# The last two modulation groups of layer 1 move from TensorE products to VectorE row sums

## The chip, the core and the metric

The kernel is written for one NeuronCore of a Trainium2 chip. TensorE (PE) multiplies matrices, VectorE (DVE) and ScalarE (ACT) work on elements, GpSimd (POOL) does some elementwise work too, and SyncE (SP) issues almost all transfers. The metric is the device time of one execution of the whole program in microseconds (us), lower being better; it is compared as the median of several executions.

## What is computed

One step of a small two-layer network over 384 tokens of width 1024: 128 context tokens and 256 latent tokens. In each layer six vectors are made from a conditioning vector, once for the context and once for the latents, and they shift, scale and gate the token stream:

```python
mod_ctx = (jax.nn.silu(c_ctx) @ w_mod[l] + b_mod[l])[None, :]
mod_lat = jax.nn.silu(c) @ w_mod[l] + b_mod[l]
...
def layer(x, mod, p, latent, kc, vc):
    sh1, sc1, g1, sh2, sc2, g2 = [m[:, None, :] for m in jnp.split(mod, 6, axis=-1)]
    h = layer_norm(x) * (1 + sc1) + sh1
    z = h @ p["w_in"] + p["b_in"]
    ...
    merged = ga * a_attn + gc * a_conv + gf * a_f
    x = layer_norm(ALPHA * x + g1 * (merged @ p["w_o"]), p["ln1_g"], p["ln1_b"])
    h = layer_norm(x) * (1 + sc2) + sh2
    u = dwconv(h @ p["w_up"], p["ffn_conv_w"], p["ffn_conv_b"])
    ug, uv = jnp.split(u, 2, axis=-1)
    x = layer_norm(ALPHA * x + g2 * ((jax.nn.silu(ug) * uv) @ p["w_down"]), p["ln2_g"], p["ln2_b"])
```

The kernel calls sh1 and sc1 group A, sh2 and sc2 group B, and g1 and g2 group G. A group of one layer is two half groups of 1024 x 1024 weights (4 MB each). `w_mod` is used for two vectors alone, so each of its 48 MB is read for very little arithmetic.

## The kernel before

All matrix products run with both operands split into a rounded part and a remainder (`whi`, `wlo`), so each product is three matmuls (`mm3`, L196 to L198). A weight block comes from memory as a `raw` tile of 1 MB (3 buffers); ScalarE rounds one half of it (`whi`, L179) and VectorE subtracts to get the remainder (`wlo`, L180), with 5 buffers of each. TensorE reads them from there.

A layer is `mixing`, then the output projection with its close, then the feed-forward loop. `mixing` runs three branches of eight steps each, in the order Fourier, attention, convolution. A step makes one gate tile (24 matmuls into a `ps` tile) and one branch tile (into an `acc` tile), and VectorE multiplies the two (L562). In the last two branches GpSimd adds the product to the merged sum (L563), and in the last one ScalarE and VectorE split that sum for the output projection (L566, L567). VectorE also runs the depthwise convolution (L785, 62 instructions a layer) and parts of the softmax in the first branches.

Modulation groups come in two ways. On TensorE (`mod_stream`, `mod_products`, L217) a group is 32 small matmuls, 64 records in the trace, in 4 steps of 16 records; they stream the weights past the two conditioning columns (`cpad`); its weights come as 32 tiles of 256 KB in `s2` buffers. On VectorE (`mod_rows`, L315) the transposed weights come as 8 tiles of 512 KB per half group, and each tile is multiplied with each of the two conditioning rows and summed along the row, two instructions a tile. The tiles pass through two `s4` buffers (of 8), and the transfer into a buffer is issued when the row sums that read it are done. Before, group A of layer 1 is made that way inside layer 0's feed-forward loop, all else on TensorE; layer 1's groups G and B run on TensorE inside layer 1's `mixing`. The conditioning rows are broadcast from a small scratch in memory, `cscr`, which setup writes.

The code is written in one order, and a scheduler fixes the order of each engine's instructions; an engine then runs its own in that order, and waits at one hold up all behind it. SP's queue is such an order as well.

Of the kernel before, what the change touches and what calls it, by code (L numbers as in the profile page):

```python
# [13 lines left out]
ALU = mybir.AluOpType  # L14
AX = mybir.AxisListType

P = 128
D = 1024
KD = D // P
DEPTH = 2  # L20
# [57 lines left out]
class Net:  # L78
# [52 lines left out]
    def setup(self):  # L131
        nc, a = self.nc, self.a
        self.zeros = self.const("zeros", [P, P])
        nc.vector.memset(self.zeros, 0.0)
        self.busy(self.WARM)
        self.ident = self.const("ident", [P, P])
        make_identity(nc, self.ident)
        self.mhalf = self.const("mhalf", [P, 1])
        nc.gpsimd.memset(self.mhalf, -0.5)
        self.zero2 = self.const("zero2", [P, 2 * KD])  # L140
        nc.gpsimd.memset(self.zero2, 0.0)
        self.cpad = self.const("cpad", [P, KD, 32])
# [12 lines left out]
        self.gscr = self.dr.tile([DEPTH, 2, 2, D], F32, tag="gscr", name="gscr", bufs=1)  # L155
        self.xscr = self.dr.tile([3, P, D], F32, tag="xscr", name="xscr", bufs=1)

    def setup_late(self):
        nc, a = self.nc, self.a
        att = self.const("att", [P, 128 + 768])  # L160
        self.load(att, a["k_att"])
        self.rope = att[:, 0:128].rearrange("p (t s c) -> p t s c", t=2, s=2)
        self.mask = att[:, 128:896].rearrange("p (t k) -> p t k", t=2)
        self.kT = [[self.sb.tile([P, 512], F32R, tag=f"kT{v}{i}", name=f"kT{v}{i}", bufs=1) for i in range(2)]
                   for v in range(NKV)]
        self.upad = [self.const(f"upad{i}", [P, UP_W]) for i in range(2)]
        for u in self.upad:
            nc.gpsimd.memset(u, 0.0)
# [124 lines left out]
                dst = self.modcol[l][:, gi, v, ks].rearrange("p (i q) -> p i q", q=ns)  # L293
                nc.vector.tensor_tensor(dst, part, bias, op=ALU.add)

    def mod_rows(self, l, kind):

        nc, a = self.nc, self.a
# [3 lines left out]
        b0 = 3 if kind == "B" else 0  # L302
        tiles = [(j, k) for j in range(2) for k in range(KD)]
        sums = [self.sm(16) for _ in range(2)]

        def fetch(n):
            j, k = tiles[n]
            self.load(w[n % 2], a["w_modr"][l - 1, self.MODS[kind], j, k])

        fetch(0)  # L310
        fetch(1)
        yield
        for n, (j, k) in enumerate(tiles):
# [3 lines left out]
            if n + 2 < len(tiles):  # L317
                fetch(n + 2)
            if k == KD - 1:
                for v in range(2):  # L320
                    nc.vector.tensor_tensor(self.modcol[l][:, j + (2 if kind == "B" else 0), v, :],
                                            sums[j][:, v * KD:(v + 1) * KD], self.bmod[l][:, j + b0, :], op=ALU.add)
            yield

    def gate_bc(self, l, j):
        out = []
# [179 lines left out]
        self.b_out(l, 1, acc, z, bb)  # L506


    def mixing(self, l, first, hT, mods):
# [23 lines left out]
        merged, m_hl = [None] * KD, []  # L533
# [36 lines left out]

        if l + 1 < DEPTH:
            self.columns(l + 1)
        mods = self.mod_stream(mods)
# [18 lines left out]
        cb = self.conv_branch(l, cT)  # L592
# [249 lines left out]
    TAIL = 5  # L842
    NF = 4

    def layer(self, l, first, hT, mods):
        nc, a = self.nc, self.a
        m_hl = self.mixing(l, first, hT, mods)
# [5 lines left out]
        for u in range(KD // 2):  # L853
            for h, w in enumerate(self.row_halves(self.raw(a["w_o"][l, u]))):
                k = 2 * u + h
# [78 lines left out]
        for u in range(KF // 2):  # L934
            ws = []
            for v in range(2):
                if 2 * u + v * KF in pre:
                    ws.append([None, None])
                else:
                    ws.append(self.halves(self.col_halves(self.raw(a["w_u"][l, u, v]))))  # L940
            for h in range(2):
                i = 2 * u + h
                cg = up_tile(i, ws[0][h])
                th = self.g()
                nc.scalar.activation(th, cg, AF.Tanh)  # L945
                nc.vector.scalar_tensor_tensor(cg, th, 1.0, cg, op0=ALU.add, op1=ALU.mult)
                cv = up_tile(KF + i, ws[1][h])
                nc.vector.tensor_tensor(cg, cg, cv, op=ALU.mult)  # L948
                hi, lo = self.r(), self.r()
                nc.scalar.copy(hi, cg)  # L950
                nc.vector.tensor_tensor(lo, cg, f32(hi), op=ALU.subtract)  # L951
                gT[i] = (hi, lo)
                if u >= 2:
                    next(rows, None)
            if u >= 1:
                down(u - 1)
        down(KF // 2 - 1)
# [47 lines left out]
    def run(self):  # L1005
# [4 lines left out]
        self.columns(0)  # L1010
        for x in xhat:
            self.norm(x, x, D)
        mods = [[(0, "G"), (0, "B")], [(1, "G"), (1, "B")]]
        first, hT = xhat, self.new_hT(0)
        for l in range(DEPTH):
            first, hT = self.layer(l, first, hT, mods[l])


@with_exitstack
# [8 lines left out]
def layout(i):  # L1028
# [30 lines left out]
    modr = g[1:][:, :, :, [0, 1]].reshape(L - 1, D, 1, 2, KD, P).transpose(0, 2, 3, 4, 5, 1)  # L1059
    kvf = cat([w_in[:, :, C_K:C_CONV], w_in[:, :, C_F:C_G]], 2)  # L1060
    up = a["w_up"]
    out = {
# [33 lines left out]
```

## Time and profile before

| what | value |
|---|---|
| median of 3 runs | 1161.87 us (1161.85 to 1164.48) |
| the profiled execution, own time | 1162.13 us |
| its span in the trace | 1160.3 us |
| PE busy | 1139.3 us (98%) |
| DVE busy | 785.1 us (68%) |
| ACT busy | 522.9 us (45%) |
| POOL busy | 77.5 us (7%) |

The span runs from the first to the last instruction of the trace, and 1.8 us of the execution's own time lie outside it. A busy share is an average over stages that have different limits, so the rows further down are read by stage. A wait is put down to the engine that ended it.

### The profile page before, as it was taken

The page shows a single profiled execution, that of the slowest core. Times are in us where ns is not written, and L with a number is a line of the kernel's source. Part 1 is how long each engine was busy: PE and PEld are TensorE (multiplying, and loading weights), DVE is VectorE, ACT ScalarE, POOL GpSimd, SP SyncE. Part 2 cuts the span into 40 slices and gives each one's busy share as a digit, 9 for nine tenths or more (in the row PEclk, how much of TensorE's full clock was granted, in tenths as well). Part 3 has the DMA queues.
Part 4 walks back from the last instruction along what each step waited for, and adds up shares of the span by engine and source line. Part 5 has one row for each costly group of instructions (what it writes and reads, how often), then busy time and mean ns, then how long its engine had stood idle before and what let it go on. Part 6 is the DMA issues. An engine that isn't in the chain of part 4 may idle for free.

```text
span 1160.3 us, 16670 instructions
## 1 busy us (share of the span) xinstructions
PE 1139.3 (98%) x6569; PEld 1019.4 (88%) x6569; DVE 785.1 (68%) x1332; ACT 522.9 (45%) x875; POOL 77.5 (7%) x91
## 2 busy tenths in 40 slices
PE   8999999999999999999999999999999999999996
PEld 6788888898999999999958978889989999999995
DVE  5579965445799976666776799444477666555667
ACT  2457743242754344444372766233447444334440
POOL 1010001121100000000021000111110000000001
PEclk9999999999999999999999999999999999999998
DMA  9764567633366663343335364783427333333411
GB/s 362 295 205 145 167 229 271 231 141 127 128 236 206 229 206 139 109 136 119 110 122 216 118 218 155 277 313 109 146 73 251 112 114 141 113 142 109 146 37 55
DMA packets 47806, 195.95 MB, mean 169 GB/s; under 512 B 5552, under 2 KB 6608, under 8 KB 32624
## 3 DMA queue, kind: packets, MB, share of 16 engines
q1 hardware_dynamic: 47296, 194.10, 47.3%
q8 instruction: 52, 0.85, 0.3%
q10 hardware_dynamic: 432, 0.79, 0.2%
q14 instruction: 26, 0.21, 0.0%
HBM read 191.41 MB, written 3.45 MB: 168 GB/s over the span
## 4 chain that ended last, share of the span: by engine, by line
PE 84%; DVE 8%; ACT 2%; DMA 2%; POOL 1%; issue 1%; SPq 0%; POOLq 0%; DVEq 0%; ACTq 0%
PE ps L196 16%; PE ps L198 16%; PE ps L197 16%; PE acc L196 9%; PE acc L197 9%; PE acc L198 9%; PE acc L217 2%; PE acc L767 1%; DVE sm L372 1%; DVE wlo L180 1%; POOL sm L376 1%; DVE s L818 1%; DVE s L828 1%; PE acc L755 1%; ACT whi L179 1%
## 5 line engine op out<-in xcount | busy, mean ns | idle before, releaser
L180 DVE TENSOR_TENSOR wlo<-raw,whi 128x1024 fp32r<-128x1024 f32 x216 | 269.1, 1247 | 236.2 <-ACT whi L179 227.2
L196 PE MATMUL ps<-hT,whi 128*128 128x386 f32 (+1 forms) x1088 | 370.3, 340 | 1.8 <-ACT g L548 1.5
L198 PE MATMUL ps<-hT,wlo 128*128 128x386 f32 (+1 forms) x1088 | 368.7, 339 | 0.0
L197 PE MATMUL ps<-hT,whi 128*128 128x386 f32 (+1 forms) x1088 | 368.4, 339 | 0.0
L179 ACT CAST whi<-raw 128x1024 fp32r<-128x1024 f32 x216 | 225.8, 1049 | 308.1 <-PE ps L197 211.4
L196 PEld LDWEIGHTS ps<-hT,whi 128*128 128x128 f32 x1088 | 205.2, 189 | 14.1 <-ACT whi L179 5.0
L197 PEld LDWEIGHTS ps<-hT,whi 128*128 128x128 f32 x1088 | 205.2, 189 | 2.7 <-issue 1.7
L198 PEld LDWEIGHTS ps<-hT,wlo 128*128 128x128 f32 x1088 | 205.3, 189 | 0.3 <-issue 0.3
L197 PE MATMUL acc<-wlo,r 128*128 128x512 f32 x360 | 142.3, 395 | 0.0
L196 PE MATMUL acc<-whi,r 128*128 128x512 f32 x360 | 142.1, 395 | 0.0
L198 PE MATMUL acc<-whi,r 128*128 128x512 f32 x360 | 141.9, 394 | 0.0
L198 PEld LDWEIGHTS acc<-whi,r 128*128 128x128 f32 x360 | 67.6, 188 | 16.2 <-DVE r L951 0.5
L196 PEld LDWEIGHTS acc<-whi,r 128*128 128x128 f32 x360 | 67.6, 188 | 14.9
L197 PEld LDWEIGHTS acc<-wlo,r 128*128 128x128 f32 x360 | 67.6, 188 | 14.4
L785 DVE SCALAR_TENSOR_TENSOR cv<-upad,cst,cv 128x399 f32<-128x399 f32 x120 | 70.1, 627 | 0.1
L376 POOL TENSOR_TENSOR sm<-sm,mhalf 128x1 f32<-128x1 f32 x21 | 23.0, 1099 | 612.4 <-DVE sm L375 611.7
L950 ACT CAST r<-g 128x386 fp32r<-128x386 f32 x44 | 22.7, 515 | 89.5 <-DVE g L948 89.5
L927 ACT ACTIVATE g<-ps,cst 128x386 f32<-128x386 f32 x84 | 56.3, 670 | 0.0
L930 DVE SCALAR_TENSOR_TENSOR g<-ps,cst,g 128x385 f32<-128x385 f32 x84 | 52.0, 619 | 2.3
L928 DVE SCALAR_TENSOR_TENSOR g<-ps,cst,g 128x385 f32<-128x385 f32 x84 | 51.6, 614 | 0.2
L563 POOL TENSOR_TENSOR g<-g,g 128x384 f32<-128x384 f32 x32 | 35.8, 1118 | 181.8 <-DVE g L562 173.3
L945 ACT ACTIVATE g<-g 128x386 f32<-128x386 f32 x44 | 23.2, 527 | 45.2 <-DVE g L930 45.2
(185 smaller groups left out, 1353.0 us busy)
## 6 DMA issues: line engine op xcount, KB each, us to landing
raw<-w_u SPq DMA_DIRECT2D x44, 1024.0 KB, 4.8
s<-w_mod SPq DMA_DIRECT2D x128, 256.0 KB, 4.4
raw<-w_g SPq DMA_DIRECT2D x24, 1024.0 KB, 7.8
raw<-w_d SPq DMA_DIRECT2D x22, 1024.0 KB, 4.9
raw<-w_mod SPq DMA_DIRECT2D x8, 1024.0 KB, 9.5
raw<-w_o SPq DMA_DIRECT2D x8, 1024.0 KB, 4.8
s<-w_modr SPq DMA_DIRECT2D x16, 512.0 KB, 4.2
s<-w_z SPq DMA_DIRECT2D x8, 512.0 KB, 9.7
```

The lines of the kernel that those rows point to most:

```text
L179: self.nc.scalar.copy(hi, raw)
L180: self.nc.vector.tensor_tensor(lo, raw, f32(hi), op=ALU.subtract)
L196: mm(ps, lh, rh, start=first, stop=False)
L197: mm(ps, lh, rl, start=False, stop=False)
L198: mm(ps, ll, rh, start=False, stop=last)
L217: self.nc.tensor.matmul(ps[32 * i:32 * i + 32, 0:n], self.cpad[:, k, :], src[k, i], start=ks[0] == 0 and k == ks[-1], stop=ks[-1] == KD - ...
L376: nc.gpsimd.tensor_tensor(mv[:, 3:4], mv[:, 2:3], self.mhalf, op=ALU.pow)
L563: nc.gpsimd.tensor_tensor(merged[m], merged[m], gt, op=ALU.add)
L785: nc.vector.scalar_tensor_tensor(c, u[:, i:i + CV_W], w, c, op0=ALU.mult, op1=ALU.add)
L927: nc.scalar.activation(c, ps, AF.Identity, bias=cols["ffn_b"][:, i:i + 1], scale=w[1])
L928: nc.vector.scalar_tensor_tensor(c[:, 1:NPAD], ps[:, 0:NPAD - 1], w[0], c[:, 1:NPAD], op0=ALU.mult, op1=ALU.add)
L930: nc.vector.scalar_tensor_tensor(c[:, 0:NPAD - 1], ps[:, 1:NPAD], w[2], c[:, 0:NPAD - 1], op0=ALU.mult, op1=ALU.add)
```

## The change

Layer 1's groups B and G are no longer made on TensorE. `mod_rows` now takes a list of half groups; half of group B joins group A in layer 0's feed-forward loop, and the other half of B and both halves of G (24 tiles, 48 row sums) are made while layer 1's attention and convolution branches run. `paced` spreads the tiles over the steps of a loop. A half of group G ends with a transpose on TensorE, a copy on ScalarE and a store into the scratch that the gate's broadcast reads. The write of `cscr` is issued later, in `setup_late`.

```diff
-        nc.sync.dma_start(self.cscr.rearrange("v (k p) -> (v k) p", p=P), ch)
+        self.silu = ch
...
     def setup_late(self):
+        nc.sync.dma_start(self.cscr.rearrange("v (k p) -> (v k) p", p=P), self.silu)
...
-    def mod_rows(self, l, kind):
+    def mod_rows(self, units):
...
-        tiles = [(j, k) for j in range(2) for k in range(KD)]
+        tiles = [(n, k) for n in range(len(units)) for k in range(KD)]
...
             for v in range(2):
-                nc.vector.scalar_tensor_tensor(prod, w[n % 2], 1.0, cb[v], op0=ALU.mult, op1=ALU.mult,
-                                               accum_out=sums[j][:, v * KD + k:v * KD + k + 1])
+                nc.vector.scalar_tensor_tensor(prod, w[i % 2], 1.0, cb[v], op0=ALU.mult, op1=ALU.mult,
+                                               accum_out=sums[n][:, v * KD + k:v * KD + k + 1])
+            if i + 2 < len(tiles):
+                fetch(i + 2)
...
+                if kind == "G":
+                    pt = self.psum("acc")[0:2 * KD, 0:P]
+                    nc.tensor.transpose(pt, sums[n], self.ident)
+                    row = self.kk()[0:2 * KD, :]
+                    nc.scalar.copy(row, pt)
+                    nc.sync.dma_start(self.gscr[l, j].rearrange("v (k p) -> (v k) p", p=P), row)
...
+    def paced(self, units, slots):
+
+        steps = self.mod_rows(units) if units else iter(())
+        need, done = len(units) * KD + 1, [0, 0]
+
+        def step():
+            done[0] += 1
+            while done[1] * slots < need * done[0]:
+                done[1] += 1
+                next(steps, None)
+
+        return step
...
+        step_rows = self.paced(rows, 14)
...
         for i, _ in enumerate(branch(1, 0, "w_a", 4, aT, lambda: values(3))):
             next(cb, None)
+            step_rows()
             if i % 2:
                 mod()
         for i, _ in enumerate(branch(2, 1, "w_c", 2, cT, lambda: [None for _ in cb])):
+            step_rows()
...
-        rows = self.mod_rows(l + 1, "A") if l + 1 < DEPTH else iter(())
+        step_rows = self.paced(rows, 17)
...
-        mods = [[(0, "G"), (0, "B")], [(1, "G"), (1, "B")]]
+        mods = [[(0, "G"), (0, "B")], []]
+        mix_rows = [[], [(1, "B", 1), (1, "G", 0), (1, "G", 1)]]
+        ffn_rows = [[(1, "A", 0), (1, "A", 1), (1, "B", 0)], []]
```

The first place is VectorE's order in layer 1's convolution branch. Before, it holds the gate product (L562, `g` times `acc`), the split of the merged sum (L567) and the remainders of the next weights (L180, `wlo`), and nothing else:

```order
L562 SCALAR_TENSOR_TENSOR g1333_7411<-g1333_7411,acc1334_7413 128x384
L567 SCALAR_TENSOR_TENSOR r1336_7423<-g1052_6016,r1335_7422 128x384
L180 TENSOR_TENSOR wlo1359_7559<-raw1357_7556,whi1358_7558 128x1024
L562 SCALAR_TENSOR_TENSOR g1338_7451<-g1338_7451,acc1339_7453 128x384
L567 SCALAR_TENSOR_TENSOR r1341_7463<-g1065_6087,r1340_7462 128x384
L180 TENSOR_TENSOR wlo1361_7563<-raw1357_7556,whi1360_7562 128x1024
```

Now the row sums (L317, into `s4`, from the tile `s41194` or `s41195` and a conditioning row) stand between them, and the numbers of the three older kinds are L586, L591 and L181:

```order
L181 TENSOR_TENSOR wlo1286_7352<-raw1284_7349,whi1285_7351 128x1024
L317 SCALAR_TENSOR_TENSOR s41193_6780,sm1197_6784<-s41195_6782,s41191_6776 128x1024
L586 SCALAR_TENSOR_TENSOR g1273_7278<-g1273_7278,acc1274_7280 128x384
L317 SCALAR_TENSOR_TENSOR s41193_6780,sm1197_6784<-s41195_6782,s41192_6778 128x1024
L591 SCALAR_TENSOR_TENSOR r1276_7290<-g1045_6027,r1275_7289 128x384
L317 SCALAR_TENSOR_TENSOR s41193_6780,sm1197_6784<-s41194_6781,s41191_6776 128x1024
L181 TENSOR_TENSOR wlo1288_7356<-raw1284_7349,whi1287_7355 128x1024
L317 SCALAR_TENSOR_TENSOR s41193_6780,sm1197_6784<-s41194_6781,s41192_6778 128x1024
```

About every second instruction of VectorE there is a row sum, from the last attention split on to the end of the branch.

The second place is TensorE at the end of that branch. Before, the last branch tile (`acc1384`) follows its gate tile (`ps1382`), and the output projection (`acc1391`) follows at once:

```order
L198 MATMUL ps1382_7696<-hT914_5332,wlo1376_7653 128x384
L196 MATMUL acc1384_7723<-r1271_7088,whi1330_7382 128x384
L197 MATMUL acc1384_7723<-r1272_7089,whi1330_7382 128x384
L198 MATMUL acc1384_7723<-r1271_7088,wlo1331_7383 128x384
L196 MATMUL acc1384_7723<-r1275_7097,whi1330_7382 128x384
L197 MATMUL acc1384_7723<-r1276_7098,whi1330_7382 128x384
L198 MATMUL acc1384_7723<-r1275_7097,wlo1331_7383 128x384
L196 MATMUL acc1391_7744<-whi1398_7752,r1335_7422 128x512
```

Now the transpose of the second half of group G (L330, from the row sums `sm1198`) stands ahead of the last two branch tiles (`acc1323` and `acc1328`):

```order
L197 MATMUL ps1326_7605<-hT915_5359,whi1319_7561 128x384
L198 MATMUL ps1326_7605<-hT916_5360,whi1319_7561 128x384
L199 MATMUL ps1326_7605<-hT915_5359,wlo1320_7562 128x384
L330 MATMUL acc1314_7550<-ident_96,sm1198_6785 16x128
L197 MATMUL acc1323_7592<-r1229_6993,whi1270_7249 128x384
L198 MATMUL acc1323_7592<-r1230_6994,whi1270_7249 128x384
L199 MATMUL acc1323_7592<-r1229_6993,wlo1271_7250 128x384
```

Twelve branch matmuls and the whole output projection have moved behind that transpose. The first half of G has such a transpose too, ahead of the second branch tile of the convolution branch.

The third place is VectorE at the same point of the change: the last row sums, then the two bias adds (L327) that the transpose waits for, and only then the last gate products:

```order
L317 SCALAR_TENSOR_TENSOR s41193_6780,sm1198_6785<-s41194_6781,s41192_6778 128x1024
L925 MEMSET ps1376_7896 128x2
L317 SCALAR_TENSOR_TENSOR s41193_6780,sm1198_6785<-s41195_6782,s41191_6776 128x1024
L925 MEMSET ps1377_7906 128x2
L317 SCALAR_TENSOR_TENSOR s41193_6780,sm1198_6785<-s41195_6782,s41192_6778 128x1024
L327 TENSOR_TENSOR sm1198_6785<-sm1198_6785,cst100_673 128x8 x2
L586 SCALAR_TENSOR_TENSOR g1322_7590<-g1322_7590,acc1323_7592 128x384
L586 SCALAR_TENSOR_TENSOR g1327_7630<-g1327_7630,acc1328_7632 128x384
```

All 48 row sums of layer 1's `mixing` thus stand ahead of the bias adds that release TensorE there.

## Rows read from the trace of the kernel before

**Rows 1.** The page, busy time, share of the span and instructions by engine.
```profile
PE 1139.3 (98%) x6569; PEld 1019.4 (88%) x6569; DVE 785.1 (68%) x1332; ACT 522.9 (45%) x875; POOL 77.5 (7%) x91
```

**Rows 2.** Windows of L217 alone: length, PE busy, PEld busy, clock, DMA.
```profile
667.70:732.80 65.10, 8.11 (x64) 1.47 (x64) 1.00 0.58 191
732.80:831.90 99.10, 7.70 (x64) 1.67 (x64) 1.00 0.58 210
```

**Rows 3.** Chain of waits around one modulation step: start, us, what.
```profile
755.94 1.85 PE acc L217 x16
757.80 0.37 PE ps L196
758.69 0.18 PE ps L197
```

**Rows 4.** Windows, all engines: PE, PEld, DVE, ACT, POOL busy, clock, DMA.
```profile
667.70:732.80 65.10, 65.05 (x420) 53.41 (x421) 58.42 (x129) 41.86 (x98) 0.53 (x1) 1.00 0.58 191
732.80:831.90 99.10, 98.71 (x585) 91.36 (x584) 45.74 (x68) 35.78 (x49) 17.61 (x18) 1.00 0.58 210
```

**Rows 5.** Timeline, DVE, layer 1's branches: start, length, instruction, wait.
```profile
722.87 1.23 DVE L180 TENSOR_TENSOR wlo<-raw,whi 128x1024 fp32r<-128x1024 f32 x1 [0.38 <-ACT whi L179]
724.01 0.63 DVE L785 SCALAR_TENSOR_TENSOR cv<-upad,cst,cv 128x399 f32<-128x399 f32 x1
...
732.23 0.56 DVE L648 TENSOR_TENSOR r<-acc,r 128x384 fp32r<-128x384 f32 x1 [1.72 <-ACT r L647]
...
788.00 0.68 DVE L282 COPY s<-acc 128x512 f32<-128x512 f32 x1
789.42 0.39 DVE L294 TENSOR_TENSOR md<-acc,cst 128x8 f32<-128x8 f32 x4 [0.75 <-PE acc L286]
...
831.39 0.55 DVE L562 SCALAR_TENSOR_TENSOR g<-g,acc 128x384 f32<-128x384 f32 x1
```

**Rows 6.** Timeline, PE, end of layer 1's convolution branch.
```profile
830.20 0.39 PE L196 MATMUL acc<-whi,r 128*128 128x512 f32 x1
```

**Rows 7.** Timeline, DVE, row sums in layer 0's feed-forward loop.
```profile
403.58 1.22 DVE L315 SCALAR_TENSOR_TENSOR s<-s,s 128x1024 f32<-128x1024 f32 x1
...
404.85 1.22 DVE L315 SCALAR_TENSOR_TENSOR s<-s,s 128x1024 f32<-128x1024 f32 x1
...
408.18 1.22 DVE L315 SCALAR_TENSOR_TENSOR s<-s,s 128x1024 f32<-128x1024 f32 x1
...
409.32 0.62 DVE L930 SCALAR_TENSOR_TENSOR g<-ps,cst,g 128x385 f32<-128x385 f32 x1
```

**Rows 8.** Tile view of w_modr: transfers from issue to landing.
```profile
DMA to landing us min/median/max: 3.6/4.2/9.4
```

**Rows 9.** Timeline, DVE, a remainder beside a GpSimd add.
```profile
740.90 1.89 DVE L180 TENSOR_TENSOR wlo<-raw,whi 128x1024 fp32r<-128x1024 f32 x1 [0.28 <-ACT whi L179]
```

**Rows 10.** Timeline, POOL, the add beside it and a slower one.
```profile
740.70 1.01 POOL L563 TENSOR_TENSOR g<-g,g 128x384 f32<-128x384 f32 x1 [5.05 <-DVE g L562]
...
811.07 1.87 POOL L563 TENSOR_TENSOR g<-g,g 128x384 f32<-128x384 f32 x1 [4.24 <-DVE g L562]
```

**Rows 11.** Windows, layer 0's feed-forward loop, with row sums and after them.
```profile
318.90:419.10 100.20, 99.87 (x548) 94.17 (x547) 96.80 (x156) 44.00 (x64) 0.00 (x0) 1.00 0.65 224
419.10:470.00 50.90, 50.90 (x267) 47.74 (x266) 31.09 (x45) 22.57 (x31) 0.00 (x0) 1.00 0.41 141
```

**Rows 12.** Timeline, SP, the first issues.
```profile
2.12 0.43 SPq L121 DMA_DIRECT2D s<-x_p  x1
5.53 0.33 SPq L154 DMA_DIRECT2D cscr<-kk  x1
```

**Rows 13.** Windows, the start: the last two columns are DMA share and GB/s.
```profile
6.00:7.00 1.00, 1.00 (x7) 1.00 (x7) 0.97 (x5) 0.00 (x0) 0.00 (x0) 1.00 0.76 277
```

**Rows 14.** Windows, TensorE's first gap: granted clock after POOL's column.
```profile
12.00:20.00 8.00, 4.03 (x66) 2.45 (x59) 5.79 (x21) 3.97 (x7) 0.55 (x1) 1.00 1.02 423
20.00:25.00 5.00, 5.00 (x42) 3.28 (x42) 1.38 (x4) 1.45 (x2) 0.00 (x0) 0.66 1.02 416
```

More of the change, by code (lines that the diff above doesn't have):

```diff
@@ L294, in mod_columns @@
                 nc.vector.tensor_tensor(dst, part, bias, op=ALU.add)
-    def mod_rows(self, l, kind):
-        nc, a = self.nc, self.a
+    def mod_rows(self, units):
+        nc = self.nc
         cb = [self.bcast(self.cscr[v]) for v in range(2)]
@@ L301, in mod_rows, with fetch @@
         w = [self.s4() for _ in range(2)]
-        b0 = 3 if kind == "B" else 0
-        tiles = [(j, k) for j in range(2) for k in range(KD)]
[L304 to L308, printed above, removed]
+        tiles = [(n, k) for n in range(len(units)) for k in range(KD)]
+        sums = [self.sm(16) for _ in units]
+        def fetch(i):
+            n, k = tiles[i]
+            l, kind, j = units[n]
+            self.load(w[i % 2], self.a["w_modr"][l, self.MODS[kind], j, k])
         fetch(0)
@@ L312, in mod_rows @@
         yield
-        for n, (j, k) in enumerate(tiles):
+        for i, (n, k) in enumerate(tiles):
             for v in range(2):
-                nc.vector.scalar_tensor_tensor(prod, w[n % 2], 1.0, cb[v], op0=ALU.mult, op1=ALU.mult,
-                                               accum_out=sums[j][:, v * KD + k:v * KD + k + 1])
-            if n + 2 < len(tiles):
-                fetch(n + 2)
+                nc.vector.scalar_tensor_tensor(prod, w[i % 2], 1.0, cb[v], op0=ALU.mult, op1=ALU.mult,
+                                               accum_out=sums[n][:, v * KD + k:v * KD + k + 1])
+            if i + 2 < len(tiles):
+                fetch(i + 2)
             if k == KD - 1:
+                l, kind, j = units[n]
+                bias = self.bmod[l][:, {"A": (0, 1), "B": (3, 4), "G": (2, 5)}[kind][j], :]
+                dst = sums[n] if kind == "G" else self.modcol[l][:, j + (2 if kind == "B" else 0)]
                 for v in range(2):
-                    nc.vector.tensor_tensor(self.modcol[l][:, j + (2 if kind == "B" else 0), v, :],
-                                            sums[j][:, v * KD:(v + 1) * KD], self.bmod[l][:, j + b0, :], op=ALU.add)
-            yield
+                    d = dst[:, v * KD:(v + 1) * KD] if kind == "G" else dst[:, v, :]
+                    nc.vector.tensor_tensor(d, sums[n][:, v * KD:(v + 1) * KD], bias, op=ALU.add)
+                if kind == "G":
[4 more added lines that the diff above has]
+                    nc.sync.dma_start(self.gscr[l, j].rearrange("v (k p) -> (v k) p", p=P), row)
+            yield
+    def paced(self, units, slots):
[7 more added lines that the diff above has]
+        return step
     def gate_bc(self, l, j):
@@ L506, in start_next, with mixing @@
         self.b_out(l, 1, acc, z, bb)
-    def mixing(self, l, first, hT, mods):
+    def mixing(self, l, first, hT, mods, rows):
         nc, a = self.nc, self.a
@@ L572, in mixing @@
             self.columns(l + 1)
-        mods = self.mod_stream(mods)
+        mods = self.mod_stream(mods) if mods else iter(())
         def mod():
             next(mods, None)
+        step_rows = self.paced(rows, 14)
         ci = conv_in()
@@ L843, with layer @@
     NF = 4
-    def layer(self, l, first, hT, mods):
+    def layer(self, l, first, hT, mods, mix_rows, rows):
         nc, a = self.nc, self.a
-        m_hl = self.mixing(l, first, hT, mods)
+        m_hl = self.mixing(l, first, hT, mods, mix_rows)
         gate = self.gate_bc(l, 0)
@@ L953, in layer @@
                 if u >= 2:
-                    next(rows, None)
+                    step_rows()
             if u >= 1:
@@ L1012, in run @@
             self.norm(x, x, D)
-        mods = [[(0, "G"), (0, "B")], [(1, "G"), (1, "B")]]
+        mods = [[(0, "G"), (0, "B")], []]
+        mix_rows = [[], [(1, "B", 1), (1, "G", 0), (1, "G", 1)]]
+        ffn_rows = [[(1, "A", 0), (1, "A", 1), (1, "B", 0)], []]
         first, hT = xhat, self.new_hT(0)
         for l in range(DEPTH):
-            first, hT = self.layer(l, first, hT, mods[l])
+            first, hT = self.layer(l, first, hT, mods[l], mix_rows[l], ffn_rows[l])
 @with_exitstack
@@ L1058, in layout @@
     mod = np.stack([g[:, :, :, [0, 1]], g[:, :, :, [3, 4]], g[:, :, :, [2, 5]]], 1)
-    modr = g[1:][:, :, :, [0, 1]].reshape(L - 1, D, 1, 2, KD, P).transpose(0, 2, 3, 4, 5, 1)
+    modr = mod.reshape(L, 3, D, 2, KD, P).transpose(0, 1, 3, 4, 5, 2)
     kvf = cat([w_in[:, :, C_K:C_CONV], w_in[:, :, C_F:C_G]], 2)
```

## The prediction

> **What bounds the kernel now.** The page comes first: PE is busy in 1139.3 of the 1160.3 us, DVE in 785.1 [rows 1]. Then the change has to be placed. The matmuls of L217 that it removes lie between 667.7 and 831.9 in layer 1's branches; I cut that at 732.8, where the split of the last attention tile ends on DVE [rows 2, 5]. The windows show PE full in both parts (65.05 of 65.1 and 98.71 of 99.1), DVE at 58.42 of 65.1 in the first and at 45.74 of 99.1 in the second [rows 4]. So TensorE is the bound in both, but in the first part DVE has 6.7 us to spare only, and in the second 53 us, into which 48 row sums are to go. The output projection begins at 830.20 [rows 6], 97.4 us after my cut; I make the sum from this distance.
>
> **What TensorE loses.** L217 is busy for 8.11 + 7.70 = 15.8 us [rows 2]. The chain shows a step of 16 records as 1.85 us, and the first matmul behind it as 0.37 where a usual one is 0.18 [rows 3]: 0.2 us more per step, 8 steps, 1.6. All in all some 17.5 us of TensorE's path, 9.5 in the first part and 8 to 9 in the second.
>
> First part: 9.5 can be won only if DVE follows. DVE's 58.42 lose the add of group G (about 0.7, the 128x512 copy's 0.68 [rows 5]) and 3.4 for two remainders and two convolution steps that now come behind the cut (2 x 1.14 and 2 x 0.55: start to start at 722.87, and 0.63 less the same overlap [rows 5]). That leaves 54.3. If DVE keeps all of its 6.7 us of idle time the part takes 61.0, a gain of 4.1; if it keeps none of what PE sets, 9.5. **I take −6.5**, nearer to the middle, since DVE's idle time there is made of short waits for ACT (0.38 and 1.72 in the rows) which shrink only in part.
>
> **What VectorE gains.** From the cut to G1's bias adds every row sum stands ahead of the transpose (L330) that TensorE must pass to reach the last two branch tiles and the output projection. So I add up DVE's time there. It has 45.74 now. Minus group B's copy and four adds, 1.1 (0.68 and 0.39 [rows 5]); minus two gate products and a split that are behind the bias adds now, 1.7 (0.55, 0.56); plus the 3.4 that came from the first part. The row sums: one is 1.22 us, and the next instruction starts 1.14 after it (408.18 to 409.32), but 1.27 when that is a row sum too (403.58 to 404.85) [rows 7]. In the new order six follow one another directly: 48 x 1.15 + 6 x 0.12 = 55.9. Six bias adds, 0.5. Sum 102.7.
>
> The Trainium skill, "VectorE: DVE Perf Modes", section "The DRAIN you can't avoid", says that the next operation does not start until the pipeline of the one before is empty, unless nothing holds it. By the rule without its exception a row sum would hold DVE to its printed end, and I estimate 5 us more for the 48. The rows at 408.18 show the exception (other work begins 0.08 us before the printed end), those of two row sums in a row the rule.
>
> Waits: a tile of 512 KB lands 3.6 to 9.4 us after its issue, 4.2 mostly [rows 8]. Two buffers with two row sums each give one tile per 2.3 us of row sums and about as much other work, so a landing of 4.2 fits mostly, not always where the order is dense; the first tile has no lead at all. **I take 4 us** of waits for tiles and for hand-offs from ACT and PE; the ends are 0, and 12 (two landings of 9.4 less 4.2, and a few of 0.5).
>
> GpSimd: the remainder at 740.90 takes 1.89 instead of 1.23, where an add of POOL had begun 0.2 us earlier, for 1.01 [rows 9, 10]; four remainders of this stretch show it, 2.6 us, and are in the 45.74. The reverse is there too: an add of POOL took 1.87 [rows 10]. So the two engines exclude each other, and whoever has begun finishes first. With DVE nearly full, 14 adds meet a busy DVE ahead of the bias adds. If all came first, DVE would stand still for 14 x 1.01 = 14.1, which is 11.5 more than now; if DVE never left a gap, 2.6 less. **I take +3.4**, nearer to the present state.
>
> The Trainium skill, "SBUF — State Buffer", section "Who interferes with whom", states that a DVE instruction with two inputs in SBUF contends with a GpSimd instruction that reads SBUF, and calls the shared ports an exclusive lock. The trace agrees (1.89 and 1.87); the full price by it is the upper end above.
>
> 102.7 + 4 + 3.4 = 110.1 to the bias adds. Then the transpose, 0.3, and twelve branch matmuls of 0.18 (the chain's usual one [rows 3]), 2.1: **112.5 us against 97.4, +15.1**. TensorE alone would need about 88 (97.4 less its own relief). It will therefore wait at this transpose for 10 us or more, the sum of all the earlier small waits included; and what is queued behind it is the rest of the branch and the whole output projection. The four removed transposes of B and the two new ones cancel within 1 us and lie inside.
>
> **Layer 0's loop.** With row sums it has PE at 99.87 of 100.2 and DVE at 96.80; behind them DVE has 31.09 in 50.9 [rows 11]. 16 more give 31.1 + 16 x 1.15 = 49.5, under 50.9. I take 0, as TensorE is full where the row sums run already. The cover is 1.4 us thin: a tile that lands 9.4 instead of 4.2 us after its issue [rows 8] could cost up to 5.
>
> **The clock.** Where TensorE had work for 4.03 of 8 us, the granted clock was 0.66 in the 5 us that followed [rows 14], that is partly the lower of its two levels. A wait of over 10 us could bring the same: 5 x 0.34 = 1.7. The ends are 0 and twice that.
>
> **The start.** SP issues the load of `x` at 2.12 and is done with it at 2.55; the store of `cscr` is issued at 5.53 [rows 12], so 3 us of SP's time pass in waiting for the vector it stores. That wait goes. But what comes behind lands in a DMA that is full: its share is 0.76 in the sixth to seventh us, the least behind that issue [rows 13], so 0.24 us are free. **−0.3**; the ends are −3.3 and 0.
>
> **Sum.** −6.5 + 15.1 + 0 + 1.7 − 0.3 = +10.0. The profiled execution took 1162.1, so 1172.1, and the median is 0.3 below it: **1172 us**.
>
> **Rivals.**
> 1. *VectorE keeps pace* (the other side). DVE streams with no gap, GpSimd waits instead, and tiles always land in time: 102.7 − 2.6 + 2.4 = 102.5 against 97.4, +5.1; the first part gives its whole 9.5, the clock nothing. 1162.1 − 9.5 + 5.1 − 0.3 = 1157; with the whole start, 1154. It decides when the last row sum ends less than some 101 us after the last attention split. For it: the order is fixed and dense, and row sums need no other engine. Against it: a remainder still waits for ACT's rounding and a gate product for PE, and the present loop with the same mix keeps 3.4 us of 100 idle [rows 11]. Chance 0.13.
> 2. *Break-even*: first part 8 to 9, the second +8 to +12: 1160 to 1165. Chance 0.15, most of it within 0.3%.
> 3. *GpSimd wins every time*: +8 on my sum, and late tiles with it: 1178 to 1186, up to 1192 with the whole 12 us of waits. For it: in this stretch it was mostly DVE that waited (four to one). Chance 0.14.
> 4. *Layer 0's loop falls behind* by the 5 us above: 1175 to 1178. Chance 0.05; it lies inside the likeliest range.
> 5. *Each row sum holds DVE for its whole length*, 1.27 from start to start as at 403.58 and not 1.14 [rows 7]: 42 x 0.12 = 5 us more, 1177. Against it stand 408.18 and most others. Chance 0.03. (It is the rule of "VectorE: DVE Perf Modes" in the Trainium skill.)
> 6. *TensorE's relief goes through whole*: 17.5 us less, 1144. It needs DVE to finish within 88 us work that sums to over 100. Chance 0.02.
>
> **How the numbers follow.** The forecast as worked out, 1166 to 1178, has 0.48; the rivals have the rest. A difference within 0.3% (3.5 us) could not be told from none by a measurement of this kernel. Faster by more is rival 1, rival 6 and little of 2: 0.15. Same is most of rival 2: 0.14. The rest, 0.71, is slower. The range 1158 to 1184 leaves out about a tenth at each end; the likeliest's own is 1166 to 1178.
>
> **What would show it.** L217 is gone from layer 1's branches, and the stretch to the last attention split is some 6 us shorter. DVE is busy in over 95% of the stretch behind it, with remainders or row sums of 1.9 us, or adds of 1.9 on POOL. PE has one wait of about 10 us or more at L330, released by DVE's bias adds (L327), with a lower granted clock behind it, and the output projection starts about 112 us after the last attention split. In layer 0's loop PE stays full. I am wrong if PE's time in the branches is spread over many waits for remainders (then DVE's lateness reaches TensorE everywhere, and the place of the transpose matters little), if TensorE reaches L330 with no wait (rival 1), or if PE loses time in layer 0's loop.

## The result

The changed kernel takes 1173.42 us (median of 4 runs, 1171.74 to 1174.37), the kernel before 1162.2 (1161.85 to 1164.48): a ratio of 1.0092, 95% interval 1.008 to 1.0104. Forecast were 1172, within 1158 to 1184. The profiled execution has a span of 1172.0 us against 1160.3.

The page, as [rows 1]: TensorE has 11.4 us less work, VectorE 73.6 us more, and the span is longer all the same.

```profile
PE 1127.9 (96%) x6439; PEld 1018.3 (87%) x6439; DVE 858.7 (73%) x1462; ACT 522.4 (45%) x877; POOL 86.6 (7%) x90
```

Where TensorE waits in layer 1's branches and output projection (us in total, times, longest):

```profile
PE acc L330 <- DVE sm L327: 21.0, 2, 17.9
PE ps L199 <- DVE wlo L181: 1.9, 2, 1.5
PE acc L828 <- DVE sm L399: 1.1, 1, 1.1
```

Both large waits are at the transposes of group G, 3.1 and 17.9 us, and the bias adds behind the row sums end them. All other waits are under 2 us.

Windows, all engines, columns as in [rows 4]: up to the last attention split, from there to the bias adds of G's second half, the 4.4 us behind them, and 50 us of layer 0's loop with row sums.

```profile
660.10:725.30 65.20, 64.48 (x394) 57.88 (x393) 60.73 (x141) 47.29 (x114) 0.00 (x0) 1.00 0.28 97
725.30:838.60 113.30, 88.67 (x496) 86.81 (x494) 104.99 (x166) 34.38 (x48) 26.74 (x17) 0.92 0.67 233
...
838.60:843.00 4.40, 4.38 (x16) 4.29 (x17) 0.99 (x2) 0.56 (x2) 1.01 (x1) 0.61 0.32 115
...
420.00:470.00 50.00, 50.00 (x263) 46.66 (x262) 46.86 (x75) 21.15 (x29) 0.00 (x0) 1.00 0.68 238
```

In the second window VectorE is busy for 105 of 113.3 us (93%) and TensorE for 88.7, the reverse of [rows 4]. Layer 0's loop keeps TensorE full.

VectorE's timeline in that window (start, length, instruction, wait): its beginning, a remainder beside a GpSimd add (the add is the last line), a wait for ScalarE, a wait for a tile, and its end.

```profile
724.73 0.56 DVE L675 TENSOR_TENSOR r<-acc,r 128x384 fp32r<-128x384 f32 x1 [0.90 <-ACT r L674]
725.20 1.21 DVE L181 TENSOR_TENSOR wlo<-raw,whi 128x1024 fp32r<-128x1024 f32 x1
726.34 0.55 DVE L586 SCALAR_TENSOR_TENSOR g<-g,acc 128x384 f32<-128x384 f32 x1
726.80 1.22 DVE L181 TENSOR_TENSOR wlo<-raw,whi 128x1024 fp32r<-128x1024 f32 x1
...
734.95 2.03 DVE L181 TENSOR_TENSOR wlo<-raw,whi 128x1024 fp32r<-128x1024 f32 x1
...
786.73 0.56 DVE L591 SCALAR_TENSOR_TENSOR r<-g,r 128x384 fp32r<-128x384 f32 x1 [1.46 <-ACT r L590]
...
835.87 1.23 DVE L317 SCALAR_TENSOR_TENSOR s<-s,s 128x1024 f32<-128x1024 f32 x1 [1.44 <-DMA s<-w_modr]
...
838.28 0.28 DVE L327 TENSOR_TENSOR sm<-sm,cst 128x8 f32<-128x8 f32 x2
...
733.97 1.93 POOL L587 TENSOR_TENSOR g<-g,g 128x384 f32<-128x384 f32 x1 [5.07 <-DVE g L586]
```

TensorE's timeline at the same point; the last row answers to [rows 6].

```profile
838.62 0.38 PE L330 MATMUL acc<-ident,sm 128*16 128x128 f32 x1 [17.93 <-DVE sm L327]
838.65 0.67 PE L197 MATMUL acc<-r,whi 128*128 128x384 f32 x1
839.12 0.52 PE L198 MATMUL acc<-r,whi 128*128 128x384 f32 x1
...
842.37 0.40 PE L197 MATMUL acc<-whi,r 128*128 128x512 f32 x1
```

The ledger of the span, after less before: layer 0's first branch matmul is 1.2 us earlier (62.87 against 64.07); layer 0's loop, from its first matmul to layer 1's first branch matmul, is as long as before (304.64 against 304.61); the last attention split ends 7.5 us earlier (725.29 against 732.79), so the first part won 6.3; from there the output projection starts after 117.1 us instead of 97.4, +19.7; from that start to the first matmul of layer 1's up-projection both take 58.44; TensorE's last matmul is 12.2 later, the span 11.7 longer.

### The profile page after: what moved, and what is told of

It is laid out like the page before. It is cut to its first block, busy times and chain, and to the rows that moved or that the text cites. A ratio compares the mean times of both kernels' runs of the same rounds, so it can differ in the third digit from the quotient of the medians.

```text
span 1172.0 us, 16503 instructions
## 1 busy us (share of the span) xinstructions
PE 1127.9 (96%) x6439; PEld 1018.3 (87%) x6439; DVE 858.7 (73%) x1462; ACT 522.4 (45%) x877; POOL 86.6 (7%) x90
## 4 chain that ended last, share of the span: by engine, by line
PE 35%; DVE 8%; issue 3%; DMA 2%; ACT 1%; POOL 1%; POOLq 0%; DVEq 0%; ACTq 0%
PE ps L197 7%; PE ps L199 7%; PE ps L198 6%; PE acc L197 4%; PE acc L198 4%; PE acc L199 4%; DVE s L317 3%; DMA s<-w_modr 2%; DVE wlo L181 1%; POOL sm L400 1%; PE acc L794 1%; PE acc L1018 1%; DVE s L845 0%; DVE sm L396 0%; DVE s L855 0%
## 5 line engine op out<-in xcount | busy, mean ns | idle before, releaser
L181 DVE TENSOR_TENSOR wlo<-raw,whi 128x1024 fp32r<-128x1024 f32 x216 | 268.9, 1247 | 184.8 <-ACT whi L180 180.3
L180 ACT CAST whi<-raw 128x1024 fp32r<-128x1024 f32 x216 | 225.9, 1049 | 308.6 <-PE ps L198 193.1
L317 DVE SCALAR_TENSOR_TENSOR s<-s,s 128x1024 f32<-128x1024 f32 x96 | 118.8, 1238 | 3.8 <-DMA s<-w_modr 3.5
L400 POOL TENSOR_TENSOR sm<-sm,mhalf 128x1 f32<-128x1 f32 x21 | 24.7, 1179 | 614.5 <-DVE sm L399 602.4
L587 POOL TENSOR_TENSOR g<-g,g 128x384 f32<-128x384 f32 x32 | 43.5, 1362 | 276.3 <-DVE g L586 272.0
```

What stands on the lines that cost most here:

```text
L180: self.nc.scalar.copy(hi, raw)
L181: self.nc.vector.tensor_tensor(lo, raw, f32(hi), op=ALU.subtract)
L317: nc.vector.scalar_tensor_tensor(prod, w[i % 2], 1.0, cb[v], op0=ALU.mult, op1=ALU.mult, accum_out=sums[n][:, v * KD + k:v * KD + k + 1])
L400: nc.gpsimd.tensor_tensor(mv[:, 3:4], mv[:, 2:3], self.mhalf, op=ALU.pow)
L587: nc.gpsimd.tensor_tensor(merged[m], merged[m], gt, op=ALU.add)
```

## The experiments

Each run is compared with the kernel before on the same chip, which takes 1162.2 to 1162.8 us there; the changed kernel's 1173.42 us, with which some runs are compared too, were measured beside 1162.2. A deferred finish means that a half of G leaves its row sums standing and gets transpose, copy and store at the place named; its transpose then goes into a `ps` tile and no longer into an `acc` tile. Where line numbers shift by a few, the lines are the same ones: the gate product is L586 or L593, a transpose of the normalised tokens L425 or L432, and so on.

**1. Both transposes late.**

```diff
         m_hl = self.mixing(l, first, hT, mods, mix_rows)
+        self.finish(0)
...
                 tail(t, n)
+        self.finish(1)
```

> All row sums stay where they are; only the two transposes of group G with their copies and stores move behind TensorE's last branch tile (first half) and behind the first part of the output projection (second half). Theory A (TensorE is held by the place of the transposes in its order): the waits of 3.1 and 17.9 us ahead of them go; the rest of the branch and the first three of eight steps of the output projection, 2.1 + 12.7 us, run in that time, and TensorE then waits some 6 to 8 us for the last splits of the merged sum, which still stand behind all row sums on VectorE. 1173.4 - 21 + 7 - 1 (clock) = about 1158, 1155 to 1162. Rival B (VectorE's sum sets the end wherever the transposes stand, through gate products, splits and remainders): the wait moves to another matmul and 1169 to 1174 remain.

Measured: 1174.63 us, ratio 1.0108 (1.0093 to 1.0123). The output projection did start at 822.50 instead of 842.37, but nothing came of it. TensorE's waits from there:

```profile
PE acc L432 <- ACT s L423: 10.6, 3, 6.1
PE acc L198 <- DVE g L593: 6.1, 1, 6.1
```

```profile
833.68 0.80 PE L198 MATMUL acc<-whi,r 128*128 128x512 f32 x1 [6.05 <-DVE g L593]
```

Six us are a wait as long as theory A foresaw, but not for a split: the output projection fills six `acc` tiles (three tiles of 128 tokens, two halves each), there are six buffers of `acc`, and the last one comes free only with the gate product (L593) of the last branch tile, which stands behind row sums. Over ten more are waits for normalised tokens in the close, which the kernel before hides. TensorE's own work from the start of the output projection to the up-projection also takes 63.5 us instead of the 57.9 of the changed kernel, at a granted clock of 0.92 against 1.00. The time is that of rival B, 0.6 above its range, but this edit has a cost of its own: the store of G's second half waited 10.3 us on SyncE's queue for the copy, ahead of loads of the close. That left the place of the transposes open.

**2. Half of B last.**

```diff
-        mix_rows = [[], [(1, "B", 1), (1, "G", 0), (1, "G", 1)]]
+        mix_rows = [[], [(1, "G", 0), (1, "G", 1), (1, "B", 1)]]
```

> The same 48 row sums and the same transposes; only the order of the half groups in layer 1's branches changes, both halves of G first and the half of B last, so that the last row sums release nothing that TensorE's branch needs. Theory A: the transposes stand earlier on both engines and cost some 3 to 6 us of waiting; the wait of 17.9 us goes, and some 6 to 8 us come back ahead of the output projection's last steps, as the splits still stand behind all row sums: 1159 to 1164. Rival B: 1169 to 1174, with the wait at the split of the merged sum instead.

Measured: 1164.27 us, ratio 1.0014 (1.0003 to 1.0024); 9 us of the 11 are gone. The same 48 row sums and both transposes are there. TensorE's waits:

```profile
PE acc L197 <- DVE g L586: 4.7, 2, 3.8
PE ps L199 <- DVE wlo L181: 2.7, 1, 2.7
...
PE acc L330 <- DVE sm L327: 1.6, 1, 1.6
PE acc L198 <- DVE wlo L181: 1.2, 1, 1.2
```

The output projection starts at 824.10 and waits in its first part for the last two gate products, which free its fifth and sixth `acc` tile, and for a remainder, not for the splits that theory A named; from its start to the up-projection it takes 67.0 instead of 58.4 us. The time is theory A's, 0.3 above its range.

**3. GpSimd's adds left out.**

```diff
-                        nc.gpsimd.tensor_tensor(merged[m], merged[m], gt, op=ALU.add)
+                        if l == 0:
+                            nc.gpsimd.tensor_tensor(merged[m], merged[m], gt, op=ALU.add)
```

> GpSimd's adds of the branch products to the merged sum are left out in layer 1, so the sum there holds the first branch alone. If their lock costs what the trace of the changed kernel shows (ten instructions of VectorE between the last attention split and the bias adds are longer by 0.5 to 0.8 us, 7 us in all), those bias adds come 7 us earlier after the last attention split (113.3 to about 106) and the time is 1166 to 1168. Rival: VectorE is held by rounding, tiles and TensorE just as long, and the time stays within 2 us of 1173.

Measured: 1166.94 us, ratio 1.004 (1.0025 to 1.0055), 6.5 less than the changed kernel. Windows from the last attention split to the bias adds, and the same remainder as at 734.95 above:

```profile
724.70:828.90 104.20, 86.67 (x496) 85.36 (x495) 97.65 (x168) 34.52 (x49) 3.53 (x3) 0.94 0.73 253
```

```profile
733.60 1.22 DVE L181 TENSOR_TENSOR wlo<-raw,whi 128x1024 fp32r<-128x1024 f32 x1
```

No instruction of VectorE is stretched any more; in the changed kernel ten were, by 7.6 us in all. VectorE's busy time falls by 7.3 and the stretch by 9.1 us; the other 1.8 are shorter waits (those for ScalarE's half of the split, 2.9, are gone, those for tiles grow from 3.0 to 5.3). The time is the one expected. The lock's price is thus shown, and that it reaches the end.

**4. Two tiles for all row sums.**

```diff
-            if i + 2 < len(tiles):
+            if i + 2 < len(tiles) and units[0][1] == "A":
```

> In layer 1's branches only the first two of the 24 tiles are loaded and every row sum reads these (the sums are not those of the weights). The three waits of VectorE for a tile there, 0.45 + 1.09 + 1.44 = 3.0 us, go. If VectorE's sum is what TensorE waits for, the time falls by 3, to about 1170.5; if a tile's wait only takes the place of a wait for ScalarE or TensorE behind it, by less than 1; if the transfers also slow the weights of the branches or VectorE itself, by 5 and more.

Measured: 1173.48 us, ratio 1.0097 (1.0082 to 1.0112). The waits for tiles are gone and the time is the same, as the second case has it. It settles less than it seems: the scheduler put the row sums earlier, the waits moved (13.2 us ahead of matmuls that need remainders, 5.5 at the transposes), and the last row sum starts at 837.00 against 837.13.

**5. Both transposes late, no store in the close.**

```diff
         m_hl = self.mixing(l, first, hT, mods, mix_rows)
+        self.finish(0)
...
+        self.finish(1)
         gate = self.gate_bc(l, 1)
```

> As the first experiment, but the second half of G gets its transpose, copy and store only ahead of the second gate's load at the end of layer 1's feed-forward loop, so that no store waits among the loads of the output projection's close. The row sums stay, in the order B, G, G. Theory A' (the place of the transposes costs what lies between the full relief and VectorE's lateness; the close was spoiled in the first experiment by the store on SyncE's queue): like the run with B last, 1162 to 1166, with some 10 to 14 us of TensorE waits left, for remainders, gate products and splits, and the store's 10 us wait on SyncE gone. Rival: the place is worth nothing and the order of the half groups gave what the second run gained: 1171 to 1175.

Measured: 1174.17 us, ratio 1.0098 (1.0081 to 1.0115). The output projection starts at 822.1, but the close's waits for normalised tokens (8.9 us) are there again without the store on the queue. Theory A' fell; the rival's time came out, not yet its reason.

**6. G's second half in layer 1's loop.**

```diff
-        mix_rows = [[], [(1, "B", 1), (1, "G", 0), (1, "G", 1)]]
-        ffn_rows = [[(1, "A", 0), (1, "A", 1), (1, "B", 0)], []]
+        mix_rows = [[], [(1, "G", 0), (1, "B", 1)]]
+        ffn_rows = [[(1, "A", 0), (1, "A", 1), (1, "B", 0)], [(1, "G", 1)]]
```

> The second half of G, used only at the end of layer 1's feed-forward loop, is made in that loop; 32 row sums remain in layer 1's branches (first half of G, then half of B), the transposes late. If VectorE's sum is the bound there: 16 x 1.15 and its share of locked adds less, 113.3 - 19.5 = 94 us against the 88 that TensorE needs, and the feed-forward loop hides the moved ones as layer 0's does: 1162.1 - 17.5 - 1.2 (start) + 5 = 1148, 1145 to 1152. Rival: remainders and gate products queue behind row sums however many there are, and the time stays over 1155; or layer 1's loop loses time (TensorE under 99% busy there).

Measured: 1155.69 us, ratio 0.9944 (0.9929 to 0.9959), 3.7 above the expected range and now faster than before. It is the rival's time, by 0.7, but not its reason: TensorE's longest wait in the branches is 1.6 us (gate activations), none there is for a remainder, and layer 1's loop shows no wait over 1.0.

**7. Row sums spread.**

```diff
+        mix_rows = [[], [(1, "G", 0)]]
+        ffn_rows = [[(1, "A", 0), (1, "A", 1), (1, "B", 0), (1, "B", 1)], [(1, "G", 1)]]
```

> All of A and B (32 tiles) in layer 0's loop, the first half of G in layer 1's branches (16 row sums), the second half in layer 1's loop. VectorE then has about 113.3 - 39 = 74 us of work where TensorE needs 88, so TensorE is the bound everywhere and its whole relief goes through: 1162.1 - 17.5 - 1.2 = 1143.4, 1141 to 1147. Rival: layer 0's loop, at 97% of VectorE for 50 us longer, falls behind: 1147 to 1152, with TensorE waits there.

Measured: 1149.9 us, ratio 0.9891 (0.9876 to 0.9906). Windows from the last attention split to the output projection:

```profile
725.90:816.60 90.70, 88.23 (x508) 87.53 (x508) 67.23 (x98) 34.41 (x48) 24.54 (x18) 1.00 0.48 164
```

TensorE is the bound again, and the branches of layer 1 are 12.9 us shorter than before (187.7 against 200.6 from their first matmul to the output projection) with 2.1 us more of waits: TensorE's relief is 15.0 us. Layer 0's loop takes 32 tiles without a wait over 0.4. The time is the rival's, its reason is not: it is not the loop that makes up the 6.5 us by which the expectation missed, but mostly the 2.5 by which I had put the relief too high and the 2.1 of waits; the last 1.9 are not accounted for.

**8. Layer 0's group G too.**

```diff
-        mods = [[(0, "G"), (0, "B")], []]
+        mods = [[(0, "B")], []]
+        mix_rows = [[(0, "G", 0)], [(1, "G", 0), (1, "B", 1)]]
+        ffn_rows = [[(0, "G", 1), (1, "A", 0), (1, "A", 1), (1, "B", 0)], [(1, "G", 1)]]
```

> As the run before last, and layer 0's group G goes the same way: its first half as 16 row sums in layer 0's branches, its second in layer 0's loop (32 tiles there in all). Another 8.5 us of TensorE's path goes; VectorE has room in layer 0's branches for 16 row sums as in layer 1's (48 were too many by 13 to 19 us, 16 leave TensorE the bound): 1148 - 8.5 = 1140, 1136 to 1144. Rival: the loads of layer 0's branches or its loop cannot take more, 1146 and over.

Measured: 1155.58 us, ratio 0.9941 (0.9926 to 0.9956), as the sixth run, far from 1140 and in the rival's range. Layer 0's branches are 6.2 us shorter, but layer 0's loop with its close is 5.3 longer, with one wait of 4.6 for a normalised tile: the second half was finished only at the loop's end, ahead of the gate that the close needs. (Run 12, with an early finish, has no such loss.)

**9. Half of B last and both transposes late.**

> The two edits of the second and the fifth run together: G, G, B, and both transposes late. Theory C (the order of the half groups is worth the 9 us, the place of the transposes nothing): 1162 to 1166, as the second run. Theory D (what lost the gain in the first and fifth run is the late finish of G's first half: its gate, loaded at 833 instead of before the output projection, and the close behind it, with TensorE waits of 9 to 11 us for the normalised tiles): 1171 to 1176, with those waits again.

Measured: 1175.39 us, ratio 1.011 (1.0094 to 1.0126): the time of theory D, and the close's waits are there (8.3 us ahead of L432). Two pieces of the chain of waits (start, us, what), the two issues of SyncE that belong to the second, and the same issues in the second run:

```profile
844.00 9.76 DMA s<-xscr
...
873.14 5.77 DMA s<-xscr
...
872.71 0.33 SPq L122 DMA_DIRECT2D raw<-w_u  x1
873.14 0.37 SPq L122 DMA_DIRECT2D s<-xscr  x1
...
849.23 13.30 SPq L121 DMA_DIRECT2D s<-xscr  x2
874.67 0.33 SPq L121 DMA_DIRECT2D raw<-w_u  x1
```

The close waits for the loads of the old tokens: the first is issued at 844.0 and lands 9.8 us later behind two weight blocks. The last is issued at 873.1, and what held it on SyncE's queue is the weight block ahead of it, for which SyncE had waited 16.5 us until 872.7. In the second run that block stands behind the last token's load, which is issued by 862.5. Runs 1 and 5 have the block ahead as well, with 14.8 and 16.5 us of waiting. So the order of the half groups is worth nothing by itself, and neither is having the transposes out of the way; the second run's gain needs its order and the early transposes together. Theory D's reason, the late gate, is not shown: the first gate's loads were issued at 832.8 (773.5 and 786.8 in the second run) and landed within 5.9 us, long before the close first stands still for a token. The late transposes come with another order of SyncE's queue. Why the scheduler chose it, and when the last token's own buffer was free, is left open.

**10. The late store alone.**

```diff
-        nc.sync.dma_start(self.cscr.rearrange("v (k p) -> (v k) p", p=P), ch)
+        self.silu = ch
...
     def setup_late(self):
...
+        nc.sync.dma_start(self.cscr.rearrange("v (k p) -> (v k) p", p=P), self.silu)
```

> The kernel before with one line of the change alone, the later store of the conditioning rows. The start as the changed kernel's trace shows it: layer 1 begins and ends 1.2 us earlier, 1161.0. By the free share of the transfers, as forecast: 0.3, 1161.9. Rival: the 1.2 us come from the schedule behind the new order and not from the store, and the time stays within 0.3 of 1162.2.

Measured: 1160.91 us, ratio 0.9985 (0.9976 to 0.9994), so 0.7 to 2.8 us. In its one trace the first branch matmul is only 0.3 earlier (63.80); over the 13 traces with the late store it lies between 62.2 and 64.6, 63.3 in the mean. The gain is there, its size not better known than that, and where it arises is not shown.

**11. Row sums over half the columns.** Half of the products in layer 1's branches are left out.

```diff
-                nc.vector.scalar_tensor_tensor(prod, w[i % 2], 1.0, cb[v], op0=ALU.mult, op1=ALU.mult,
+                m = D if units[0][1] == "A" else D // 2
+                nc.vector.scalar_tensor_tensor(prod[:, 0:m], w[i % 2][:, 0:m], 1.0, cb[v][:, 0:m], op0=ALU.mult, op1=ALU.mult,
```

> The changed kernel with the 48 row sums of layer 1's branches taken over the first 512 of 1024 columns only (half of these products is left out); tiles, loads, transposes and order of the groups stay. If VectorE's sum sets the end of the stretch, 48 x 0.55 = 26 us less leave 113.3 - 26 = 87, less than TensorE's 88, so that the waits at the transposes go almost entirely: 1173.4 - 21 - 1.6 (clock) = 1150 to 1154, near the 1149.9 of the seventh run. Rival (the transposes, loads or hand-offs as such are the cost): over 1160.

Measured: 1156.94 us, ratio 0.995 (0.9931 to 0.9968), between what was expected and the rival. The stretch to the bias adds fell from 113.3 to 90.9 us, 0.47 for each of the 48 row sums, although VectorE now waits 8.1 us for tiles there (3.0 in the changed kernel). TensorE's waits fell with it. The window of that stretch and the waits:

```profile
724.80:815.70 90.90, 83.37 (x472) 82.71 (x470) 76.66 (x161) 31.89 (x45) 19.76 (x17) 0.98 0.80 268
...
PE acc L331 <- DVE sm L328: 7.7, 2, 4.5
PE ps L197 <- ACT g L573: 0.7, 1, 0.7
```

Thirteen of the 21 us are gone with nothing but the length of the row sums. The rest, 7.7, I had expected to go. How much of it is the place of the transposes and how much those waits for tiles is not shown.

**12. Both layers, finished early.**

```diff
+        mods = [[(0, "B")], []]
+        mix_rows = [[(0, "G", 0)], [(1, "G", 0)]]
+        ffn_rows = [[(0, "G", 1), (1, "A", 0), (1, "A", 1), (1, "B", 0), (1, "B", 1)], [(1, "G", 1)]]
...
                     self.pending.append((l, j, sums[n]))
+                    if j == 1:
+                        self.finish(1)
...
         m_hl = self.mixing(l, first, hT, mods, mix_rows)
+        self.finish(0)
```

> Best of the runs so far (all of A and B in layer 0's loop, the halves of G in layer 1's branches and loop) with layer 0's group G made the same way, and the halves made in a loop finished as soon as their sums stand, so that no gate is late. Layer 0's branches were 6.2 us shorter with such a group; layer 0's loop now has 40 tiles, which VectorE takes until about its end. 1149.9 - 6.2 = 1143.7 if the loop holds them, 1142 to 1146; if it falls behind or the last layer norm waits, 1147 to 1153.

Measured: 1142.56 us, ratio 0.9827 (0.9813 to 0.9841), as expected and faster than both kernels. Layer 0's loop with 40 tiles, as [rows 11]:

```profile
318.00:570.00 252.00, 252.00 (x1314) 235.29 (x1313) 238.55 (x381) 103.52 (x143) 1.46 (x1) 1.00 0.63 212
```

TensorE has no gap there in 252 us, with VectorE busy for 95%.

## Why the prediction was right, and where its terms were off

**The step that decided** held: the row sums ahead of G's bias adds are more than VectorE can do while TensorE does the branches, and TensorE stands at the transpose in front of the output projection. The forecast had 10 us or more there; 17.9 and 3.1 came. That VectorE's amount is the cause is shown from two sides: less of it by shorter row sums (run 11) and by unlocked instructions (run 3) shortens the stretch by 22.4 and 9.1 us, and with two thirds of the row sums gone TensorE is the bound again (run 7, whose late transposes gain nothing by themselves in runs 1 and 5).

**VectorE's sum.** From the cut to the bias adds 113.3 us were measured, 110.1 forecast. Apart: the work with no lock is 97.4 (104.99 less 7.6), where I had 100.1 (102.7 less 2.6). The row sums come out at the 55.9 forecast (from start to start, less their part of the lock); the 2.7 less are the older instructions, which I took over at the length that they have alone, 1.23 for a remainder and 0.55 for a gate product [rows 5], while back to back they take 1.14 and 0.46 from start to start (725.20 to 726.34 to 726.80). The waits are 8.3 where I took 4: 3.0 for tiles, 2.9 for ScalarE's half of the split, 1.1 each for GpSimd's step of a normalisation (L400) and for TensorE. This was the worst-sized term, and its larger part are hand-offs, for which I had counted next to nothing. The lock with GpSimd adds 4.9 to the old 2.6, where I took 3.4; the ends were −2.6 and 11.5. Remainders and row sums of 1.85 to 2.04 us stand beside adds of 1.9 (734.95 and 733.97 above), so both engines pay. With more waits than forecast VectorE is busy in 93% of the stretch, not in the over 95% that was named as a sign.

**The lower clock**: +1.7 forecast. The granted clock is 0.61 in the 4.4 us behind the wait of 17.9 us, so mostly the lower of its two levels, and the twelve branch matmuls take 3.7 us instead of 2.1, +1.6; the dip that [rows 14] shows at the start came here too.

**The first part**: −6.5 forecast, −6.3 measured. **Layer 0's loop**: 0 and 0.0; run 12 shows that even 40 tiles fit. **The start**: −0.3 was too little; the ledger has −1.2, and run 10 gives a gain of 0.7 to 2.8 for the late store alone.

**The total** is closer than its terms, and that is luck in part: against the measured ones the work was 2.7 too high, the waits 4.3 and the lock 1.5 too low, and the start gave 0.9 more than forecast.

**TensorE's relief** was put at 17.5 us and is 15.0 (run 7). The 0.2 us behind each step of [rows 3] should not have been added to the busy time of L217: eight steps of 1.85 + 0.2 by the chain are 16.4, and what was measured is below even the 15.8 of [rows 2]. The rest of the difference isn't settled; the two transposes and other order of the new kernel are in it. In the second part the 88 us for TensorE alone held: it is busy for 88.2 there in run 7. The relief only moved the bounds here, and the expectations of runs 6 to 8.

**What the prediction had too simple** is what lies behind the transpose. It counted the branch's end and the output projection as held by it, which they are, but not what moving it would give. Runs 1, 5 and 9 moved it: the output projection starts 20 us sooner and the time stays, because its first part waits 6.1 us for a gate product that also stands behind row sums, and the close then waits for tokens that come late. Only the half of B last with early transposes (run 2) returned 9 us, which leaves that kernel 2 us above the one before.

**The rivals.** The first needed the last row sum less than 101 us after the last attention split; it ended after 113. Break-even needed 8 to 12 us in the second part, which lost 19.7. GpSimd winning every time would have cost 11.5, and 4.9 came; the 1192 named as that rival's upper end counts the 4 us of waits twice, 1172 + 8 + 8 is 1188. The rule of the Trainium skill on the shared ports ("SBUF — State Buffer", "Who interferes with whom") is borne out by run 3: with no adds, no stretched instruction. The Trainium skill, "VectorE: DVE Perf Modes", section "The DRAIN you can't avoid", lets a next operation start earlier when nothing holds it. The changed kernel shows what the one before did: a remainder starts 1.14 us after a row sum of 1.22, a second row sum only 1.25 to 1.27 after the first.

## What to carry to other kernels

Work that goes from a full engine to one with spare time has to fit the stretch that releases it, hand-offs and locks included: add up the receiving engine from a fixed point to the instruction that the full engine waits for, and compare with what the full engine needs there. Ask for each part when its result is first used; here a third of what was put into the branches was not needed before the end of the next loop, another third could be made in the loop before, and with the row sums spread by need the same idea gave 1.1% instead of costing 0.9% (run 7), and 1.7% with layer 0's group G as well (run 12). A wait that stands alone in the profile need not be worth its length: with the transposes moved away, its time came back as waits for other results of the late engine and for loads that the new order of the queues put late.

## What was not expected

A GpSimd add of 128x384 costs up to 0.8 us of the VectorE instruction that meets it (2.03 against 1.22), close to its own 1.01 when alone; the kernel before showed 0.66 [rows 9]. Tiles landed about as fast as before, although 24 of them are now loaded in layer 1's branches: those whose landing the trace tells (11 of the 24) take 3.4 to 5.8 us with a median of 4.0, at 233 GB/s in the stretch, against 3.6 to 9.4 with a median of 4.2 before [rows 8]. So the 3.0 us that VectorE waits for tiles come without any landing near 9.4 that the trace shows.
